# A scaled copy in which most weights are loaded behind the first store, and the first two input tiles are cut differently

## The chip, the cores and the metric

The kernel runs on one core of a Trainium2 chip. A core has several engines with instruction streams of their own: VectorE (DVE), ScalarE (ACT), GpSimd (POOL), SyncE (SP) and TensorE (unused here). Data moves between the chip's main memory (HBM) and the on-chip memory (SBUF, 128 partitions) by DMA: SyncE and ScalarE issue transfers, each into a queue of its own, and 16 DMA engines work both queues off. The metric is the time of one execution on the device in microseconds; lower is better.

## The reference

Every token is a row of 512 numbers and has two weights. The output holds for each token the row times the first weight and the row times the second. The expert indices are not used.

```python
x:              (16, 1024, 512) float32      # 33.6 MB
expert_weights: (16, 1024, 2)   float32      # 0.13 MB
x_expanded = x[:, :, np.newaxis, :].repeat(k, axis=2)     # k = 2
return x_expanded * expert_weights[..., np.newaxis]       # 67.1 MB
```

For each byte read two are written, and one multiplication is made for each output number.

## The kernel before

The 16,384 tokens are laid over 128 partitions, 128 tokens for each. They are cut into five tiles of 25 tokens per partition (L32) and a rest of three (`LAST`, L34). A tile of input is 128 x 51,200 bytes, 6400 KB. Two input buffers exist (`x_pool`, L44), one output buffer for a whole tile (`o_ring`, L48), one small tile for the last three tokens (`z_tile`, L58), and one for all weights (`w_tile`, L47): 256 columns, two for each token.

**Loads.** `load(i)` (L68) issues the input of tile i on ScalarE's queue. Tile 0 comes in two transfers of 9 and 16 tokens (`FIRST`, L35), every other tile in one. Right behind the first transfer of tile 0 the function issues the weights on SyncE's queue in three loads (L95, L97, L104): those of tile 0 (25 KB), of tiles 1 to 4 (100 KB) and of the rest (3 KB). In SBUF a partition's weights of one tile are 200 bytes, so these loads consist of many 200-byte pieces, while a partition's share of an input tile is one piece of 51,200 bytes. Behind tile 0's second transfer comes the input of the last three tokens (L85), then tile 1.

**Products.** `emit` (L148) goes through a tile in parts: the first two tiles in parts of 13 and 12 tokens, the others in 9, 8 and 8 (L157). Each part is filled by `fill` (L142): VectorE takes the first `v` tokens of a part in chunks of up to four (one TENSOR_TENSOR for each, L127), ScalarE the rest with one ACTIVATE for each token and weight (L117). `SHARES` (L36) gives `v`; for the first two tiles ScalarE has four tokens of each part, from the third tile on it has none. When a part is filled, SyncE issues its store (L152).

**Order.** Each engine runs its instructions in the order written. A wait on SyncE or ScalarE holds back every issue behind it on the same engine. The framework adds the waits: a product waits for its input, its weights and for the store that last read its part of `o_ring`; a load into an input buffer waits until all products of the tile that held it before are done. The main loop (L154 to L159) issues loads 0 and 1, then for each tile the products and stores, followed by the load two tiles ahead, on ScalarE behind its products. The last three tokens end the kernel (L160).

Of the kernel before, what the change touches and what calls it, by code (L numbers as in the profile page):

```python
# [1 line left out]

# [4 lines left out]


@with_exitstack
def kernel(  # L10
    ctx: ExitStack,
    tc: tile.TileContext,
    x: bass.AP,
    expert_indices: bass.AP,
    expert_weights: bass.AP,
    out: bass.AP,
):
    nc = tc.nc

    batch, seq, hidden = x.shape  # L20
    k = expert_weights.shape[-1]
    P = nc.NUM_PARTITIONS
    ntok = batch * seq
    assert ntok % P == 0
    A_TOTAL = ntok // P

    f32 = mybir.dt.float32
    row = k * hidden
    CH = 4


    groups = [25, 25, 25, 25, 25]  # L32
    TX = max(groups)
    LAST = 3  # L34
    FIRST = [9, 16]  # L35
    SHARES = [[9, 8], [9, 8], [9, 8, 8]]  # L36
    assert sum(groups) + LAST == A_TOTAL

    xf = x.rearrange("b s h -> (b s) h")
    of = out.rearrange("b s k h -> (b s) (k h)")  # L40
    wf = expert_weights.rearrange("b s k -> (b s) k")

    w_pool = ctx.enter_context(tc.tile_pool(name="w_pool", bufs=1))
    x_pool = ctx.enter_context(tc.tile_pool(name="x_pool", bufs=2))  # L44
    o_pool = ctx.enter_context(tc.tile_pool(name="o_pool", bufs=1))

    w_tile = w_pool.tile([P, A_TOTAL * k], f32)  # L47
    o_ring = o_pool.tile([P, TX * row], f32)  # L48

    def rows(of_all, done, T):  # L50
        return of_all[done * P : (done + T) * P, :].rearrange(
            "(p a) n -> p (a n)", a=T
        )


    if LAST:
        z_pool = ctx.enter_context(tc.tile_pool(name="z_pool", bufs=1))
        z_tile = z_pool.tile([P, LAST * hidden], f32)  # L58

    tiles = []  # L60
    done = 0
    for n in groups:
        tiles.append((done, n))
        done += n

    loaded = []

    def load(i):  # L68
        if i >= len(tiles):
            return  # L70
        done, n = tiles[i]
        x_tile = x_pool.tile([P, TX * hidden], f32)
        src = rows(xf, done, n)
        steps = FIRST if i == 0 else [n]
        for e, step in enumerate(steps):
            at = sum(steps[:e])
            nc.scalar.dma_start(
                out=x_tile[:, at * hidden : (at + step) * hidden],
                in_=src[:, at * hidden : (at + step) * hidden],
            )  # L80
            if i == 0 and e == 0:
                for g in range(3):
                    weights(g)
        if i == 0 and LAST:
            nc.scalar.dma_start(out=z_tile, in_=rows(xf, A_TOTAL - LAST, LAST))  # L85
        loaded.append(x_tile)


    T0 = groups[0]
    G = len([n for n in groups[1:] if n == T0])  # L90
    head = (1 + G) * T0

    def weights(e):
        if e == 0:
            nc.sync.dma_start(out=w_tile[:, : T0 * k], in_=rows(wf, 0, T0))  # L95
        elif e == 1:
            nc.sync.dma_start(  # L97
                out=w_tile[:, T0 * k : head * k].rearrange("p (g n) -> p g n", g=G),
                in_=wf[T0 * P : head * P, :].rearrange(
                    "(g p a) n -> p g (a n)", g=G, p=P  # L100
                ),
            )
        else:
            nc.sync.dma_start(  # L104
                out=w_tile[:, head * k :], in_=rows(wf, head, A_TOTAL - head)
            )

    def product(engine, o_tile, t, x_in, c, m):

        o = t * row  # L110
        if engine is not None:
            for e in range(m * k):
                out_e = o_tile[:, o + e * hidden : o + (e + 1) * hidden]
                in_e = x_in[:, e // k * hidden : (e // k + 1) * hidden]
                w_e = w_tile[:, c + e : c + e + 1]
                if engine is nc.scalar or engine is nc.any and (c + e) % 3 == 2:
                    nc.scalar.mul(out=out_e, in_=in_e, mul=w_e)  # L117
                else:
                    nc.vector.tensor_scalar(
                        out=out_e,  # L120
                        in0=in_e,
                        scalar1=w_e,
                        scalar2=None,
                        op0=mybir.AluOpType.mult,
                    )
            return
        nc.vector.tensor_tensor(  # L127
            out=o_tile[:, o : o + m * row].rearrange(
                "p (t k h) -> p t k h", t=m, k=k
            ),  # L130
            in0=x_in[:, : m * hidden]
            .rearrange("p (t h) -> p t h", t=m)
            .unsqueeze(2)
            .to_broadcast([P, m, k, hidden]),
            in1=w_tile[:, c : c + m * k]
            .rearrange("p (t k) -> p t k", t=m)
            .unsqueeze(3)
            .to_broadcast([P, m, k, hidden]),
            op=mybir.AluOpType.mult,
        )  # L140

    def fill(o_tile, x_in, c, m, v):  # L142
        for t in range(0, v, CH):
            u = min(t + CH, v)
            product(None, o_tile, t, x_in[:, t * hidden : u * hidden], c + t * k, u - t)
        product(nc.scalar, o_tile, v, x_in[:, v * hidden :], c + v * k, m - v)

    def emit(src, dst, c, cuts, shares):  # L148
        for at, to, v in zip(cuts, cuts[1:], shares):
            o_tile = o_ring[:, at * row : to * row]  # L150
            fill(o_tile, src[:, at * hidden : to * hidden], c + at * k, to - at, v)
            nc.sync.dma_start(out=dst[:, at * row : to * row], in_=o_tile)  # L152

    for i in range(2):  # L154
        load(i)
    for i, (done, n) in enumerate(tiles):
        cuts = [0, 13, n] if i < 2 else [0, 9, 17, n]  # L157
        emit(loaded[i], rows(of, done, n), done * k, cuts, SHARES[min(i, 2)])
        load(i + 2)  # L159
    emit(  # L160
        z_tile,
        rows(of, A_TOTAL - LAST, LAST),
        (A_TOTAL - LAST) * k,
        [0, LAST],
        [LAST],
    )

# [1 line left out]
_INS = ['x', 'expert_indices', 'expert_weights']  # L169
_OUTS = [((16, 1024, 2, 512), 'float32')]  # L170


# [23 lines left out]
```

## Time and profile before

| what | before |
|---|---|
| time, median of 3 runs | 239.54 us (239.51 to 239.99) |
| the profiled execution: its time, its span | 240.12 us, 238.3 us |
| bytes read from HBM, written | 33.69 MB, 67.11 MB |
| mean rate over the span | 423 GB/s |
| stores of 6656 KB, 6144 KB (median from issue to landing) | 33.1 us, 44.5 us |

The span runs from the first to the last instruction that the profiler recorded; some time of an execution lies outside it. "Issue to landing" of a transfer holds its wait in the queue as well as its movement. In the lines of issues, ACTq and SPq are the instruction streams of ScalarE and SyncE that issue transfers: the time beside them is that of the issue, and the movement itself comes later.

### The profile page before, as it was taken

What the parts mean: (1) busy time and instruction counts of PE and PEld (TensorE: products, weight loads), DVE (VectorE), ACT (ScalarE), POOL (GpSimd) and SP (SyncE); (2) the same over time, 40 slices, a digit from 0 to 9 for tenths busy, and PEclk for the clock granted to TensorE, in tenths of its full rate; (3) what the DMA queues carried; (4) which work ended last, traced back from release to release, by engine and by line L of the source; (5) the groups of instructions that cost most, each with busy time, mean ns of one, the idle gap of its engine ahead of it and who ended that gap; (6) DMA issues with size and microseconds to landing.
All of it is one profiled execution on the core that took longest, in us unless ns stands there. A gap on an engine that the chain in (4) does not pass through costs nothing.

```text
span 238.3 us, 167 instructions
## 1 busy us (share of the span) xinstructions
DVE 122.6 (51%) x32; ACT 21.2 (9%) x33; POOL 0.2 (0%) x4
## 2 busy tenths in 40 slices
DVE  0599600000069292099405999493086999865000
ACT  0008900000061250000000000000000000000000
POOL 0000000000000000000000000000000000000000
DMA  7999999999999999999999999999999999999996
GB/s 264 465 386 504 457 414 413 413 424 429 429 396 429 472 465 426 422 404 405 412 484 431 402 434 444 414 434 425 449 408 461 434 440 431 421 413 423 440 434 264
DMA packets 3840, 100.80 MB, mean 423 GB/s; under 512 B 1152, under 2 KB 1152, under 8 KB 1280
## 3 DMA queue, kind: packets, MB, share of 16 engines
q1 hardware_dynamic: 2832, 67.24, 65.5%
q10 hardware_dynamic: 1008, 33.55, 33.2%
HBM read 33.69 MB, written 67.11 MB: 423 GB/s over the span
## 4 chain that ended last, share of the span: by engine, by line
DMA 58%; DVE 28%; issue 2%; another core or an unknown queue 2%; ACT 1%; DVEq 0%; SPq 0%
DMA out_dram<-o_ring 55%; DVE o_ring L127 28%; DMA x_tile<-in_x_dram 3%; ACT o_ring L117 1%; DVEq L127 0%; SPq L152 0%
## 5 line engine op out<-in xcount | busy, mean ns | idle before, releaser
L127 DVE TENSOR_TENSOR o_ring<-x_tile,w_tile 128x4096 f32<-128x4096 f32 (+1 forms) x31 | 119.3, 3905 | 93.2 <-DMA out_dram<-o_ring 82.3
L117 ACT ACTIVATE o_ring<-x_tile,w_tile 128x512 f32<-128x512 f32 x32 | 19.9, 708 | 47.1 <-DMA out_dram<-o_ring 47.0
L127 DVE TENSOR_TENSOR o_ring<-z_tile,w_tile 128x3072 f32<-128x3072 f32 x1 | 3.4, 3359 | 2.1 <-DMA out_dram<-o_ring 2.1
L117 ACT ACT_TABLE_LOAD x1 | 1.3, 1283 | 18.7 <-DMA x_tile<-in_x_dram 18.7
L180 POOL MEMSET const-uint8-127<- 128x1 uint8 x1 | 0.1, 102 | 0.0
L180 POOL MEMSET const-bfloat16-1.0<- 128x1 bf16 x1 | 0.1, 101 | 0.0
L180 POOL MEMSET const-float32-0.0<- 128x1 f32 x1 | 0.1, 98 | 0.2 <-issue 0.2
L180 POOL MEMSET const-float32-1.0<- 128x1 f32 x1 | 0.1, 98 | 0.0
## 6 DMA issues: line engine op xcount, KB each, us to landing
x_tile<-in_x_dram ACTq DMA_DIRECT2D x4, 6400.0 KB, 31.6
out_dram<-o_ring SPq DMA_DIRECT2D x6, 4096.0 KB, 21.5
out_dram<-o_ring SPq DMA_DIRECT2D x3, 4608.0 KB, 27.3
out_dram<-o_ring SPq DMA_DIRECT2D x2, 6656.0 KB, 33.1
out_dram<-o_ring SPq DMA_DIRECT2D x2, 6144.0 KB, 44.5
x_tile<-in_x_dram ACTq DMA_DIRECT2D x1, 4096.0 KB, 17.5
x_tile<-in_x_dram ACTq DMA_DIRECT2D x1, 2304.0 KB, 8.1
out_dram<-o_ring SPq DMA_DIRECT2D x1, 1536.0 KB, 19.5
```

What stands on the lines that cost most here:

```text
L117: nc.scalar.mul(out=out_e, in_=in_e, mul=w_e)
L127: nc.vector.tensor_tensor(out=o_tile[:, o : o + m * row].rearrange("p (t k h) -> p t k h", t=m, k=k), in0=x_in[:, : m * hidden] .rearrange ...
L180: nc = _bacc.Bacc("TRN2", target_bir_lowering=False, num_devices=1)
```

## The change

Tile 0 comes in one load and tile 1 in two, of 16 and 9 tokens; the input of the last three tokens follows behind tile 1. The first weight load covers tiles 0 and 1 (50 KB). The other two, of tiles 2 to 4 (75 KB) and of the rest (3 KB), are issued on SyncE behind the first store. To hold them there, ScalarE copies some columns of the input tile into the part of `w_tile` that these loads fill afterwards: the loads must wait for that copy, and the copy stands behind ScalarE's products of the first part. The values copied are overwritten and used by nobody. The shares change too: VectorE takes 7 tokens of each part of tile 0 (ScalarE 6 and 5), and 10 and 9 of tile 1 (ScalarE 3 and 3).

```diff
-    FIRST = [9, 16]
-    SHARES = [[9, 8], [9, 8], [9, 8, 8]]
+    STEPS = {1: [16, 9]}
+    SHARES = [[7, 7], [10, 9], [9, 8, 8]]
...
-        steps = FIRST if i == 0 else [n]
+        steps = STEPS.get(i, [n])
...
             if i == 0 and e == 0:
-                for g in range(3):
-                    weights(g)
-        if i == 0 and LAST:
+                weights(0)
+        if i == 1 and LAST:
             nc.scalar.dma_start(out=z_tile, in_=rows(xf, A_TOTAL - LAST, LAST))
...
     def weights(e):
-        if e == 0:
-            nc.sync.dma_start(out=w_tile[:, : T0 * k], in_=rows(wf, 0, T0))
-        elif e == 1:
+        if e < 2:
+            at, to = ((0, 2 * T0), (2 * T0, head))[e]
+            g = (to - at) // T0
             nc.sync.dma_start(
-                out=w_tile[:, T0 * k : head * k].rearrange("p (g n) -> p g n", g=G),
-                in_=wf[T0 * P : head * P, :].rearrange(
-                    "(g p a) n -> p g (a n)", g=G, p=P
+                out=w_tile[:, at * k : to * k].rearrange("p (g n) -> p g n", g=g),
+                in_=wf[at * P : to * P, :].rearrange(
+                    "(g p a) n -> p g (a n)", g=g, p=P
                 ),
             )
...
             nc.sync.dma_start(out=dst[:, at * row : to * row], in_=o_tile)
+            if c == 0 and at == 0:
+                nc.scalar.copy(
+                    out=w_tile[:, 2 * T0 * k :],
+                    in_=src[:, : (A_TOTAL - 2 * T0) * k],
+                )
+                weights(1)
+                weights(2)
```

## The prediction

> **What bounds the kernel now.** I read the page first: engine shares, the slices and the queues.
>
> ```profile
> DVE 122.6 (51%) x32; ACT 21.2 (9%) x33; POOL 0.2 (0%) x4
> DMA  7999999999999999999999999999999999999996
> DMA packets 3840, 100.80 MB, mean 423 GB/s; under 512 B 1152, under 2 KB 1152, under 8 KB 1280
> q1 hardware_dynamic: 2832, 67.24, 65.5%
> q10 hardware_dynamic: 1008, 33.55, 33.2%
> ```
>
> No compute engine is busy much over half the span, while the 16 DMA engines are full in every slice but the first and the last. Queue q10 carries ScalarE's loads, q1 what SyncE issues: stores and weights. Together they take 98.7% of the engines' time. The split of the span into stages says where the other 1.3% lies (columns: stretch, length, busy time and count for DVE, ACT and POOL, clock, DMA share, GB/s).
>
> ```profile
> 0.00:3.00 3.00, 0.00 (x0) 0.00 (x0) 0.20 (x4) 1.00 0.39 104
> 3.00:20.00 17.00, 11.17 (x4) 1.26 (x1) 0.00 (x0) 1.00 1.06 449
> 20.00:50.00 30.00, 7.45 (x2) 9.93 (x17) 0.00 (x0) 1.00 1.00 421
> 50.00:92.00 42.00, 18.66 (x5) 10.01 (x16) 0.00 (x0) 1.00 1.00 434
> 92.00:150.00 58.00, 36.30 (x10) 0.00 (x0) 0.00 (x0) 1.00 1.00 428
> 150.00:236.00 86.00, 49.05 (x13) 0.00 (x0) 0.00 (x0) 1.00 1.00 431
> 236.00:238.30 2.30, 0.00 (x0) 0.00 (x0) 0.00 (x0) 1.00 0.10 43
> ```
>
> From 3 to 236 us the share is 1.00: the kernel is a transport of fixed bytes at the engines' full rate, with a ramp of about 1.8 us lost ahead (61% of 3 us) and 2.1 behind (90% of 2.3). A wait of DVE, ACT or a store costs nothing as long as either queue still holds work. Only three things can move the end: the ramp, the engine time per byte, and a moment in which both queues are empty.
>
> What lies in the queues early is read from the issues in order of time and their landings (last number: us from issue to landing; the second 6400 KB row is the third tile's load, issued at 29.97).
>
> ```profile
> 0.73 0.89 ACTq L77 DMA_DIRECT2D x_tile<-in_x_dram  x2
> 0.73 0.38 SPq L95 DMA_DIRECT2D w_tile<-in_expert_weights_dram  x1
> 1.64 0.52 ACTq L85 DMA_DIRECT2D z_tile<-in_x_dram  x1
> 2.19 0.81 ACTq L77 DMA_DIRECT2D x_tile<-in_x_dram  x1
> 25.07 193.26 SPq L152 DMA_DIRECT2D out_dram<-o_ring  x14
> 29.97 0.37 ACTq L77 DMA_DIRECT2D x_tile<-in_x_dram  x1
> x_tile<-in_x_dram ACTq DMA_DIRECT2D x1, 2304.0 KB, 8.1
> w_tile<-in_expert_weights_dram SPq DMA_DIRECT2D x1, 25.0 KB, 5.3
> w_tile<-in_expert_weights_dram SPq DMA_DIRECT2D x1, 100.0 KB, 36.7
> x_tile<-in_x_dram ACTq DMA_DIRECT2D x1, 6400.0 KB, 33.8
> x_tile<-in_x_dram ACTq DMA_DIRECT2D x1, 6400.0 KB, 21.8
> out_dram<-o_ring SPq DMA_DIRECT2D x1, 6656.0 KB, 42.4
> ```
>
> A 100 KB load needs 36.7 us. The packets by queue in the stretch from 20 to 36 us say why:
>
> ```profile
> q10 hardware_dynamic: 155, 6.86, 99.5%
> q1 hardware_dynamic: 154, 0.03, 1.0%
> ```
>
> 155 pieces of input went by, and 154 small pieces of SyncE's queue: each engine takes **one piece from each queue in turn**, whatever its size. Each transfer has one piece for each of 128 partitions, 8 per engine; the weights are 8+32+8 = 48 per engine. These stand before the first store in SyncE's queue. So the store issued at 25.07 cannot move until the third tile's load has landed (29.97+21.8 = 51.8), and it lands at 67.5. The reader should see that this block is real but free: the engines carry loads meanwhile.
>
> The Trainium skill, "DMA: Bandwidth & Descriptors", section "Queues, rings and completion order", lets an engine drain a whole packet, some 9 to 17 descriptors, before it changes queue; by that the weights would pass in a few turns. The 155 against 154 speaks against it here.
>
> **The change, part by part.** Bytes and packets first. Before: 7 loads, 3 weight loads, 14 stores. After: 7 loads (tile 0 in one, tile 1 in two), 3 weight loads, 14 stores, with 16, 24 and 8 weight pieces per engine in place of 8, 32 and 8. Pieces per engine and bytes are equal: **0**. The ramp: the first load and first weight load are both issued at 0.73 as before: **0**.
>
> The one price that shows in the queue rows is that loads run less smoothly than stores: 67.24 MB in 65.5% of 238.3 us is 431 GB/s, 33.55 MB in 33.2% is 424. At the stores' rate the loads would need 77.9 us rather than 79.1, so **1.2 us** is the whole excess. It cannot be placed from these rows, but stages that start or mix loads show lower rates. The change adds a mixed stage (the first store meets the second tile's pieces) and moves others. Ends: -1.2 if all excess went, +1.2 if it doubled; I take +0.1, near nothing, since from the fourth load on everything meets the same partners as before.
>
> Now the schedule, as that decides whether a queue runs empty. Prices of compute:
>
> ```profile
> L127 DVE TENSOR_TENSOR o_ring<-x_tile,w_tile 128x4096 f32<-128x4096 f32 x26 | 113.8, 4421 | 93.2 <-DMA out_dram<-o_ring 82.3 <-DMA x_tile<-in_x_dram 8.8 <-issue 2.1
> L127 DVE TENSOR_TENSOR o_ring<-x_tile,w_tile 128x1024 f32<-128x1024 f32 x5 | 6.1, 1219 | 0.0
> L127 DVE TENSOR_TENSOR o_ring<-z_tile,w_tile 128x3072 f32<-128x3072 f32 x1 | 3.4, 3359 | 2.1 <-DMA out_dram<-o_ring 2.1
> 18.74 1.28 ACT L117 ACT_TABLE_LOAD   x1 [18.74 <-DMA x_tile<-in_x_dram]
> 20.03 9.91 ACT L117 ACTIVATE o_ring<-x_tile,w_tile 128x512 f32<-128x512 f32 x16
> ```
>
> *The first tile in one load.* Its bytes are the same, so it lands at 18.7, as its second part did (18.74); the loss is DVE's early start at 8.8. *The first weight load* now has 16 pieces and a completion mark per engine, 17 turns. How many pass before input starts moving? In the old profile a 2304 KB load is 8 pieces of 0.70 us (2.359 MB at 424 GB/s, an eighth); it landed at 8.8, the weights at 6.0, so some 4 of the 8 turns lay behind them. Of 9 weight turns, 4 alternated and 5 went ahead. With 5 ahead again, 12 alternate: 8 with the first tile's pieces, 1 with its completion mark, 3 with the second tile's 32 KB pieces (4.194 MB at 424 GB/s, an eighth: 1.24 us). So the weights land not with the tile but at 18.7 + 3 x 1.24 = **22.4**, and all of DVE and ACT waits for them. The table load lies under that wait.
>
> *New shares.* Seven tokens on DVE: 4.42 + 3.36 = 7.8 us; six on ACT: 12 x 0.62 = 7.4. First store issued at 30.2 rather than 25.07. ScalarE's queue holds the first two tiles and the last three tokens, 13.9 MB as before, until the old landing of the second tile, 2.19 + 33.8 = 36.0; I take 35.4 for the last byte moved (an estimate). From an issue to its first piece:
>
> ```profile
> 0.73 8.08 DMA x_tile<-in_x_dram
> q10 hardware_dynamic: 4, 0.07, 66.0%
> q1 hardware_dynamic: 44, 0.01, 18.0%
> ```
>
> The last two rows are the stretch from 1.5 to 2.0 us, in which the first four input pieces and 44 of SyncE's moved: 0.8 to 1.3 us behind the issue at 0.73, I take 1.1. The store moves from 31.3: **cover of 4 us** is left. Cost 0.
>
> *Copy and late weights.* The copy writes 156 columns on ACT, between none and 0.62 us (one 512-column ACTIVATE); I take 0.3, as 156 is under a third. A change of table there and back would add 2 x 1.28. Behind it on ACT stand ten products (6.2 us) and the issue of the third tile's load. ACT ends at 29.8 + 0.3 + 6.2 = 36.3, at most 39.2; DVE ends its second seven tokens at 30.2 + 7.8 = 38.0. SyncE waits for the copy with two small loads, and the second store is queued behind them, ready only at 38.0 anyway. The third tile's load is issued at about 38, not 29.97; the first store covers it: **0**, and if it were not there, 38.0+1.1-35.4, some 4 us, would be idle.
>
> *What is late next.* The first store's 6.82 MB take 15.8 us at 431 GB/s; in its 8 turns it meets three 18 KB pieces (0.70 each) and five of the last tokens' pieces (0.23): 31.3 + 15.8 + 2.1 + 1.2 = 50.4, against 67.5 before. DVE's ten tokens of tile 1 (2 x 4.42 + 2.3, between the 1219 and the 3359 row) end at 61.5. The late weights again alternate with 8 big pieces, now the third tile's (15.5 us, to 67), then 25 small ones pass, then the second store (6.29 MB, 14.6 us) lands near 82. Before:
>
> ```profile
> 67.59 9.90 DVE o_ring L127 x3
> 77.49 4.48 another core or an unknown queue
> 82.06 8.77 DVE o_ring L127 x2
> 90.89 0.36 ACTq L77 DMA_DIRECT2D x_tile<-in_x_dram  x1
> ```
>
> There the second store freed its half at 82.0 too. So the 17 us won at the first store are given back in a longer wait for the second. Tile 1's second half: 9 tokens, 9.9 us, and the fourth load is issued near 92 against 90.89; the third store (15.8 us from 82) covers it with 6 us to spare. From there the two kernels are alike.
>
> **Sum:** 238.3 + 0 + 0 + 0.1 = 238.4 of span, about 240.2 for the execution, which took 240.12 with 1.8 outside its span. The median of the runs is 239.54, 0.6 lower; differences are added to that: **239.6**.
>
> **Rivals.** *Starved (slower).* The first store waits for weights, and the weights for turns. If no weight piece goes ahead of the input on one engine (their generation takes longer with 16 pieces than with 8, and all 16 engines must finish), 17 turns alternate: five more of 1.24 us, landing at 28.6, first store moving at 37.5, and both queues are empty from 35.4: 2.1 us, all lost. With one ahead it is 0.9; from two ahead on nothing. Time 240.4 to 241.6, middle 241.1. For it: the pieces double and the lead was only 5. Against it: 44 of SyncE's pieces against 4 of input moved from 1.5 to 2.0 us. Chance 0.20.
>
> *Switching dearer (slower).* Store and load meet once more, and the excess of 1.2 us over five large loads grows by half or more: +0.6 to +1.2, 240.3. Against it: the stretch 92 to 150, where loads mix with stores, still shows 428 GB/s. Chance 0.13.
>
> *Smoother loads (faster).* The big pieces at the beginning and the small weights out of the way remove half or all of the excess: -0.6 to -1.2, 238.7. For it: the stretch 20 to 50 has the lowest rate of the middle, 421, and is the one that changes. Against it: the same number of weight pieces still alternates with input. Chance 0.15.
>
> *It does not do what it says.* If weights pass many to a turn, they land with the tile, the first store is issued at 26.5, and nothing starves either. By the rule of the Trainium skill ("DMA: Bandwidth & Descriptors", the section above) this is what happens. Same 239.6; it is held in the forecast.
>
> **How the numbers follow.** A measurement of this kernel can tell about 0.2% (0.48 us) from no change. Forecast, no change: 0.52, between 239.1 and 240.0. Slower 0.20 + 0.13 = 0.33, faster 0.15. For 8 in 10 the range reaches to 238.9 (most of the smooth case, whose full end is 238.3) and to 241.6 (the end of the starved case).
>
> **What would show it.** Right: DMA share of 1.00 in every stage from 3 to 236 us; DVE's first instruction near 22.5, some 4 us after the tile has landed; the first store landing near 50, the second near 82; the fourth load issued near 92. Starved: DVE's first instruction past 27 and a hole in the DMA slices near 36. Smoother or dearer: shares of 1.00 but q10's share of time below 32.8% or above 33.5% for the same 33.55 MB. I would be wrong altogether if the ramp moved: a first slice other than 7.

## The result, and the profile after

| | before | after |
|---|---|---|
| median of 5 runs each | 239.56 us (239.51 to 239.99) | 246.44 us (246.38 to 250.33) |
| ratio to before, 95% interval | 1 | 1.0292 (1.0267 to 1.0317) |
| execution shown: time, span | 240.12, 238.3 us | 246.35, 244.2 us |

The changed kernel is 2.9% slower: 6.9 us, where the forecast was 239.6 us and the range ended at 241.6. The first profile of the changed kernel was taken in a disturbed execution of 250.33 us, so the rows of "after" come from a repeat of the same kernel (run e16 below).

The page of the changed kernel, first: engine shares, slices, queues.

```profile
span 244.2 us, 174 instructions
DVE 121.5 (50%) x32; ACT 22.7 (9%) x36; POOL 0.2 (0%) x4
DMA  7999969799999999999999999999999999999995
DMA packets 3840, 100.80 MB, mean 413 GB/s; under 512 B 1152, under 2 KB 1152, under 8 KB 1280
q1 hardware_dynamic: 2832, 67.24, 64.5%
q10 hardware_dynamic: 1008, 33.55, 32.5%
```

Packets and bytes are those of before, to the digit. The engines work 97.0% of 244.2 us, 236.9 us in all, against 98.7% of 238.3, 235.2. So 4.2 of the 5.9 us of span are time in which engines stand still, and the rest is longer engine time for the same bytes. The slices show where to look: a 6 in the sixth and a 7 in the eighth, from 30 to 49 us, and a 5 in the last. The split into stages is sharper (columns as in the prediction):

```profile
0.00:3.00 3.00, 0.00 (x0) 0.00 (x0) 0.20 (x4) 1.00 0.88 273
3.00:34.00 31.00, 5.13 (x2) 5.14 (x8) 0.00 (x0) 1.00 0.96 410
34.00:36.00 2.00, 2.00 (x1) 2.00 (x4) 0.00 (x0) 1.00 0.53 215
36.00:38.30 2.30, 2.30 (x2) 2.30 (x5) 0.00 (x0) 1.00 0.00 0
38.50:60.00 21.50, 5.67 (x2) 5.45 (x9) 0.00 (x0) 1.00 1.03 402
60.00:236.00 176.00, 106.19 (x28) 7.57 (x12) 0.00 (x0) 1.00 1.00 431
```

A row credits a piece to the stretch in which it begins, with its whole time and bytes, so a share can pass 1, and the edges of a stretch shift its rate; the rate divided by the share is free of that.

From 36.0 to 38.3 us no piece begins (by the trace's records the last one had ended at 35.7), and both compute engines are busy throughout. This is the moment of two empty queues that the prediction named as one of three things that could move the end. From 60 us on the rate is 431 GB/s, as before: nothing is won or lost there until the last microseconds. The stretch between, 38.5 to 60, has full engines (1.03) and yet moves 402 GB/s, where before it was 427 at 1.02:

```profile
38.50:60.00 21.50, 0.00 (x0) 0.00 (x0) 0.00 (x0) 1.00 1.02 427
```

Divided by the share that is 390 against 419 GB/s. The timeline says what was late:

```profile
0.73 1.39 ACTq L77 DMA_DIRECT2D x_tile<-in_x_dram  x3
0.73 0.44 SPq L96 DMA_DIRECT2D w_tile<-in_expert_weights_dram  x1
28.84 1.28 ACT L116 ACT_TABLE_LOAD   x1 [28.84 <-DMA w_tile<-in_expert_weights_dram]
28.87 15.30 DVE L126 TENSOR_TENSOR o_ring<-x_tile,w_tile 128x4096 f32<-128x4096 f32 x4 [28.87 <-DMA w_tile<-in_expert_weights_dram]
37.62 0.35 SPq L151 DMA_DIRECT2D out_dram<-o_ring  x1
44.26 0.36 ACTq L77 DMA_DIRECT2D x_tile<-in_x_dram  x1
64.28 10.96 DVE L126 TENSOR_TENSOR o_ring<-x_tile,w_tile 128x4096 f32<-128x4096 f32 x3 [20.11 <-DMA out_dram<-o_ring]
88.18 9.90 DVE L126 TENSOR_TENSOR o_ring<-x_tile,w_tile 128x4096 f32<-128x4096 f32 x3 [12.94 <-issue]
98.16 49.17 ACTq L77 DMA_DIRECT2D x_tile<-in_x_dram  x2
```

The bracket behind DVE's first instruction reads: idle for 28.87 us, and a weight load ended it. The chain of waits has the same (start, us, what):

```profile
0.73 28.04 DMA w_tile<-in_expert_weights_dram
28.87 15.31 DVE o_ring L126 x4
44.23 28.81 DMA out_dram<-o_ring
```

A load of 50 KB is on the path for 28 us. The packets by queue, first from 1.5 to 2.0 us, say how it began:

```profile
q10 hardware_dynamic: 11, 0.56, 374.9%
```

There is no row for q1: eleven input pieces had begun, and not one piece of weights. From 5 to 15 us:

```profile
q10 hardware_dynamic: 81, 4.15, 95.7%
q1 hardware_dynamic: 81, 0.02, 0.8%
```

One for one again. Sixteen pieces and a completion mark, each behind a big piece of input: no weight piece went ahead. The Trainium skill, "DMA: Bandwidth & Descriptors", section "Queues, rings and completion order", lets an engine drain a whole packet of some 9 to 17 descriptors before it changes queue; 81 against 81 does not agree with it, and by it the weights would have landed with the first tile or before it.

### The profile page after: what moved, and what is told of

Its sections match the earlier page's. It is cut to its first block, busy times and chain, and to the rows that moved or that the text cites. A ratio compares the mean times of both kernels' runs of the same rounds, so it can differ in the third digit from the quotient of the medians.

```text
span 248.2 us, 174 instructions
## 1 busy us (share of the span) xinstructions
DVE 121.5 (49%) x32; ACT 22.7 (9%) x36; POOL 0.2 (0%) x4
## 4 chain that ended last, share of the span: by engine, by line
DMA 68%; DVE 19%; issue 4%; SPq 0%; DVEq 0%
DMA out_dram<-o_ring 57%; DVE o_ring L126 19%; DMA w_tile<-in_expert_weights_dram 11%; SPq L151 0%; DVEq L126 0%
## 5 line engine op out<-in xcount | busy, mean ns | idle before, releaser
L126 DVE TENSOR_TENSOR o_ring<-x_tile,w_tile 128x4096 f32<-128x4096 f32 (+3 forms) x31 | 118.1, 3869 | 104.2 <-DMA out_dram<-o_ring 52.8
L116 ACT ACTIVATE o_ring<-x_tile,w_tile 128x512 f32<-128x512 f32 x34 | 21.3, 708 | 40.2 <-DMA out_dram<-o_ring 40.2
L116 ACT ACT_TABLE_LOAD x1 | 1.3, 1283 | 28.8 <-DMA w_tile<-in_expert_weights_dram 28.8
## 6 DMA issues: line engine op xcount, KB each, us to landing
out_dram<-o_ring SPq DMA_DIRECT2D x6, 4096.0 KB, 22.4
```

The lines of the kernel that those rows point to most:

```text
L126: nc.vector.tensor_tensor(out=o_tile[:, o : o + m * row].rearrange("p (t k h) -> p t k h", t=m, k=k), in0=x_in[:, : m * hidden] .rearrange ...
```

## The experiments

Each was compared with runs of the kernel before on the same chip; those medians were 240.03 to 240.22 us. "Slower" in the text means that the interval of the ratio lies above 1.

### Is it the late weights?

**e5** repeats the changed kernel beside three variants; **e6** issues the first weight load on ScalarE's queue, ahead of the first tile; **e7** issues all three weight loads at the start, without the copy; **e8** leaves the kernel before as it is and only gives ScalarE ten tokens in place of four in the first tile's second part, so that the third tile's load is issued late.

> The changed kernel itself. If its first weight load is always late (16 pieces that all wait behind input pieces), DVE's first instruction is again near 29 us and both queues are empty from about 36 to 38.5; 246 to 247 us. If that was chance, some executions are near 243, what the version with two first weight loads takes.

e6, against the changed kernel:

```diff
+            if i == 0 and e == 0:
+                weights(0, nc.scalar)
             nc.scalar.dma_start(
...
-            if i == 0 and e == 0:
-                weights(0)
...
```

> The changed kernel with its first weight load (two tiles, 16 pieces) on ScalarE's queue ahead of the first input, so that no input piece can stand before it. Weights land by 4 us, tile 0 by 19.5, the first store is issued near 27, no hole. 'Empty queues' as the whole cause: 239.5 to 240.5. What the split weights showed (242.3 to 243.7 without the hole): half of the loss comes from elsewhere, so 242 to 244 again.

e7, against the changed kernel:

```diff
-                weights(0)
+                for g in range(3):
+                    weights(g)
...
-            if c == 0 and at == 0:
-                nc.scalar.copy(
-                    out=w_tile[:, 2 * T0 * k :],
-                    in_=src[:, : (A_TOTAL - 2 * T0) * k],
-                )
-                weights(1)
-                weights(2)
```

> The changed kernel with its two later weight loads at the start, behind the first one, and no copy. If the first load's 16 pieces lose their turn to the 51,200-byte input pieces whatever follows them: DVE starts near 29 us, the hole is there, 245 to 247. If they go ahead, as 18,432-byte pieces let them in the kernel before: no hole, 241 to 243 like the single first load alone.

e8, against the kernel before:

```diff
-    SHARES = [[9, 8], [9, 8], [9, 8, 8]]
+    SHARES = [[9, 2], [9, 8], [9, 8, 8]]
```

> The kernel before with only one number changed: in tile 0's second part VectorE takes 2 tokens and ScalarE 10, so that the third tile's load is issued near 37.4 instead of 30 us, when ScalarE's queue has just run dry (near 36) and the first store has begun to move. No moment with both queues empty. Theory 'load queue running dry costs' (the engines stall when a load comes into an empty queue beside moving stores): 241 to 243, with the stalls between 37 and 45 us. 'Only empty queues cost': 239.5 to 240.3.

| | median (range), runs | ratio (95%) | DVE begins |
|---|---|---|---|
| e5 | 246.45 (245.94 to 247.09), 4 | 1.0259 (1.0224 to 1.0294) | 28.80 |
| e6 | 242.32 (241.31 to 243.39), 4 | 1.0086 (1.0039 to 1.0134) | 19.57 |
| e7 | 245.52 (245.16 to 246.02), 4 | 1.0220 (1.0188 to 1.0252) | 28.74 |
| e8 | 239.98 (239.72 to 240.27), 4 | 0.9988 (0.9958 to 1.0018) | 8.84 |

All four ran on one chip. With the weights ahead of the input, 4.1 us of the loss are gone (246.45 - 242.32). Moving the other weight loads back to the start gives at most a microsecond; the intervals of e5 and e7 overlap. In e8 the stage from 38.5 to 60 us reads

```profile
38.50:60.00 21.50, 0.00 (x0) 0.00 (x0) 0.00 (x0) 1.00 1.00 433
```

Its third tile's load was issued at 37.5 instead of 29.97, into a queue that had run dry, while a store moved, and nothing was lost. So an empty load queue alone does no harm. e6 also shows a rest: with no hole (no moment of two empty queues) the kernel is still 0.9% slower than before, 2.3 us.

### The parts alone

Five variants of the kernel before, each with one or two parts of the change. **e2**: only the first weight load covers two tiles. **e4**: only the late weights (those of tiles 1 to 4 and the rest, behind the first store). **e11**: only the first tile in one load. **e12**: only the second tile in two pieces. **e10**: only the new shares of the second tile.

e2, against the kernel before; e4 has the changed kernel's copy and late loads, from column `T0 * k` on:

```diff
-        if e == 0:
-            nc.sync.dma_start(out=w_tile[:, : T0 * k], in_=rows(wf, 0, T0))
-        elif e == 1:
+        if e < 2:
+            at, to = ((0, 2 * T0), (2 * T0, head))[e]
+            g = (to - at) // T0
...
```

> The kernel before, with only its first weight load widened to two tiles (16 pieces per engine) and the second narrowed to three; all weights still at the start, input as before. Both theories: the first weights land near 18 us instead of 6 if none of the 16 goes ahead of the input (near 13 if five do), DVE starts that much later, second part of tile 0 done near 37.6; the queue of loads lasts to 36 and the first store then stands ready, so no hole: 239.5 to 240.0. More than 241 would say that the late start costs by another way than empty queues.

> The kernel before with only the late weights of the change: tile 0's weights at the start (8 pieces), those of tiles 1 to 4 and of the rest behind the first store, held by the copy; input and shares as before. First store issued near 25 and moving from about 26 while the loads still run to 36 and longer: no hole, but early mixing. 'Empty queues': 239.5 to 240.0. 'Mixing': 241.5 to 243.5.

e11:

```diff
-    FIRST = [9, 16]
-    SHARES = [[9, 8], [9, 8], [9, 8, 8]]
+    FIRST = [25]
+    SHARES = [[7, 7], [9, 8], [9, 8, 8]]
```

> The kernel before with only tile 0 in one load and shares of 7 and 7 for it; tile 1 in one load behind the last three tokens, its shares as before, weights at the start. 'Shares': 239.6 to 240.5. 'Cut of the input', if it is the single first load: 241.5 to 243.

e12 (and the last three tokens' load behind tile 1):

```diff
-    FIRST = [9, 16]
+    STEPS = {0: [9, 16], 1: [16, 9]}
...
-        steps = FIRST if i == 0 else [n]
+        steps = STEPS.get(i, [n])
```

> The kernel before with only tile 1 in loads of 16 and 9 tokens and the last three tokens behind it; all else as before. 'Shares': 239.6 to 240.5. 'Cut of the input', if it is the second tile's cut or the small load of the last tokens beside the first store: 241.5 to 243.

e10:

```diff
-    SHARES = [[9, 8], [9, 8], [9, 8, 8]]
+    SHARES = [[9, 8], [10, 9], [9, 8, 8]]
```

> The kernel before with only tile 1's shares changed to 10 and 9. 'Shares': 241.5 to 243, stalls near 95 to 102. 'Cut of the input': 239.6 to 240.3.

| | median (range), runs | ratio (95%) |
|---|---|---|
| e2 | 240.14 (239.58 to 242.58), 10 | 1.0020 (0.9993 to 1.0048) |
| e4 | 239.86 (239.62 to 240.29), 10 | 0.9992 (0.9980 to 1.0005) |
| e11 | 240.24 (239.99 to 241.15), 10 | 1.0008 (0.9989 to 1.0028) |
| e12 | 242.98 (240.30 to 251.23), 4 | none: runs 240.30, 240.45, 245.51, 251.23 |
| e10 | 241.03 (240.26 to 242.24), 10 | 1.0039 (1.0015 to 1.0063) |

e4 and e11 cost nothing: late weights with their copy, and the first tile in one load, are free. In e4 the first store moves beside the loads as early as 26 to 34 us (22 of its pieces begin there), so the early mixing that its expectation and that of e1 name as a rival is not the cause either. e2 costs nothing either, but there DVE began at 9.30 and the 50 KB had landed in 8.5 us: on that chip, beside a first input load of nine tokens, the bigger weight load did go ahead, so e2 says nothing of the step in question. e12 stays open: two of its four runs are far off, the other two are near the kernel before.

The surprise is e10. Moving two tokens of the second tile from ScalarE to VectorE costs 1.0 us (241.03 - 240.07, the kernel before on that chip), though ScalarE is idle for nine tenths of the time and VectorE for nearly half of it. The time lies between the two ranges of the expectation: the shares cost something, but less than was thought. The last two stages of e10,

```profile
236.00:237.00 1.00, 0.00 (x0) 0.00 (x0) 0.00 (x0) 1.00 0.35 148
237.00:240.00 3.00, 0.00 (x0) 0.00 (x0) 0.00 (x0) 1.00 0.03 12
```

and of the kernel before,

```profile
236.00:237.00 1.00, 0.00 (x0) 0.00 (x0) 0.00 (x0) 1.00 0.24 98
237.00:240.00 3.00, 0.00 (x0) 0.00 (x0) 0.00 (x0) 1.00 0.00 0
```

differ in a thin tail: a share of 0.03 over 3 us is as much as one engine of sixteen for 1.4 us (0.03 x 3 x 16). The other engines have ended by then. Why the shares of an early tile make one engine late at the end is not settled.

### Combinations

**e3** has the input cuts and the shares of the change with the weights as before; **e9** is e3 with the old shares [9, 8] of the second tile. **e1** is the changed kernel with the first weight load as two loads of one tile; **e14** is e1 with the old shares.

e3, against the kernel before; e9 has [9, 8] for [10, 9]:

```diff
-    FIRST = [9, 16]
-    SHARES = [[9, 8], [9, 8], [9, 8, 8]]
+    STEPS = {1: [16, 9]}
+    SHARES = [[7, 7], [10, 9], [9, 8, 8]]
...
-        if i == 0 and LAST:
+        if i == 1 and LAST:
```

> The kernel before with only the input and the shares of the change: tile 0 in one load, tile 1 in 16 and 9 tokens, the last three tokens behind it; weights in three loads at the start as before. 'Empty queues': tile 0's weights (8 pieces) land by about 10 to 19 us, first store issued near 27.5, third input load issued near 34.3, before the loads run out: 239.5 to 240.0. 'Mixing': the small weights again hold the first store back until the third tile has landed, so no early mixing: 239.5 to 240.0 too. Over 241 would say that the single first load costs by itself.

> The kernel of e3 (input and shares of the change, all weights at the start), but with tile 1's shares as before (VectorE 9 and 8 tokens, not 10 and 9). Theory 'shares': with 9 tokens DVE needs 9.9 us for tile 1's second part instead of 8.8, so the fourth load and the fourth store are issued about 1 us later beside the third store, and that is where e3 stalled (95 to 102 us); then 239.6 to 240.5 here. Rival 'cut of the input' (one big first load, or tile 1 in two): 241.5 to 243 as e3.

e1, against the changed kernel:

```diff
-                weights(0)
+                weights(0, 0, T0)
+                weights(0, T0, 2 * T0)
...
```

> The changed kernel, its first weight load (16 small pieces per DMA engine) issued as two loads of one tile each (8 pieces, then 8). Theory 'empty queues' (the time is lost while neither queue holds work, because the first products wait for 16 pieces that move one per input piece): tile 0's weights need 9 turns at most, so they land by about 19 us; the first store is issued near 27.5 and moves long before the loads end near 35.5; no hole; 239.5 to 240.0 us. Rival 'mixing' (stores that move while loads still run slow both, and that is half of the loss or more): the hole is gone, but stores still meet loads early, so 242.5 to 243.5.

> The changed kernel with both repairs: its first weight load in two loads of one tile each (no hole) and tile 1's shares as before. If lateness of the weights and the new shares are all that costs: 240.0 to 240.8, the same as before within 0.3%. If single big loads or weights behind the first store cost too: 241.5 or more.

| | median (range), runs | ratio (95%) |
|---|---|---|
| e3 | 242.31 (240.79 to 246.28), 8 | 1.0090 (1.0054 to 1.0126) |
| e9 | 240.50 (239.82 to 242.21), 10 | 1.0021 (0.9996 to 1.0047) |
| e1 | 243.22 (242.29 to 243.74), 4 | 1.0128 (1.0097 to 1.0159) |
| e14 | 241.92 (240.01 to 244.71), 4 | 1.0102 (1.0031 to 1.0172) |

e3 is slower than the kernel before by 0.9%, and e9 with the old shares cannot be told from it. That points to the shares again, but e3 and e9 ran on different chips and e3's runs scatter over 5 us, so the 1.8 us between them are no measure of the price. e1 has no hole (DVE begins at 18.90) and is 3.2 us faster than the changed kernel, but still slower than before; in e14 the runs scatter too far to say whether the old shares help there. e1 and e14 ran on chips on which a two-tile load went first as well (e2, e13), so their times don't show that splitting it is what put the weights ahead.

### Who goes first, and what it costs

**e13** is the changed kernel with the old shares of the second tile. It ran on a chip on which the weights went ahead. **e16** and **e17** are the changed kernel and e13 once more, side by side on another chip. **e18** is e13 with the 3 KB weight load ahead of the first one on SyncE, so that the first weights are forced to come later.

e13 (and e17), against the changed kernel:

```diff
-    SHARES = [[7, 7], [10, 9], [9, 8, 8]]
+    SHARES = [[7, 7], [9, 8], [9, 8, 8]]
```

> The changed kernel with tile 1's shares as before (VectorE 9 and 8 tokens, not 10 and 9); the late first weights stay. If the empty queues and the stalls right behind them cost about 4 us and the new shares some 2: DVE starts near 29 us, the hole near 36 is there, 243.5 to 244.8. If the empty queues are nearly all of it: 245.5 to 246.5. If the shares are the larger part: 242 to 243.

> The changed kernel once more, on the same chip and beside e17, which differs in tile 1's shares alone. In its traces so far the first input piece moved at 1.79 us and no weight piece before 4.1; in the kernel of e13 the weights went first at 1.77 and the input at 1.95, though both issue the same two first transfers at the same time. If who goes first belongs to the program (a few nanoseconds in its start): weights late again, hole near 36, 246 to 247. If it belongs to the chip: as e17 beside it, 242 to 243.5 if the weights go first on this chip.

> The changed kernel with tile 1's old shares, once more. If who goes first belongs to the program: weights first, DVE from about 19.4 us, no hole, 240.5 to 242. If it belongs to the chip and the input goes first on this one: DVE from about 29, hole near 36, 243.5 to 245.

e18, against e13:

```diff
+                weights(2)
                 weights(0)
...
-                    out=w_tile[:, 2 * T0 * k :],
-                    in_=src[:, : (A_TOTAL - 2 * T0) * k],
+                    out=w_tile[:, 2 * T0 * k : head * k],
+                    in_=src[:, : (head - 2 * T0) * k],
                 )
                 weights(1)
-                weights(2)
```

> The changed kernel with tile 1's old shares and the first weight load made late for certain: the 3 KB load of the last weights stands ahead of it on SyncE's queue, so its issue begins some 0.45 us behind the first input load. Its 16 pieces per engine then all wait behind input pieces: DVE from 29 to 31 us, first store issued near 38 to 40, both queues empty from about 36 for 3 to 5 us. If the hole and the restart behind it are the larger part of the loss: 243.5 to 246.5. If late weights cost little and the new shares are the cause: 240.5 to 242.

| | median (range), runs | ratio (95%) | DVE begins |
|---|---|---|---|
| e13 | 241.35 (240.48 to 242.30), 10 | 1.0040 (1.0018 to 1.0062) | 19.41 |
| e16 | 246.64 (246.35 to 247.08), 4 | 1.0266 (1.0240 to 1.0292) | 28.87 |
| e17 | 245.69 (245.62 to 245.95), 4 | 1.0227 (1.0204 to 1.0250) | 28.83 |
| e18 | 247.87 (247.63 to 247.99), 4 | 1.0314 (1.0291 to 1.0337) | 30.89 |

e13 and e17 are the same program, 4.3 us apart, while the kernel before took 240.22 and 240.20 us on the two chips. The timeline of e13 has DVE wait for the weights only until 19.41:

```profile
19.41 15.30 DVE L126 TENSOR_TENSOR o_ring<-x_tile,w_tile 128x4096 f32<-128x4096 f32 x4 [19.41 <-DMA w_tile<-in_expert_weights_dram]
28.16 0.35 SPq L151 DMA_DIRECT2D out_dram<-o_ring  x1
```

and its packets from 1.5 to 2.0 us read

```profile
q10 hardware_dynamic: 3, 0.15, 95.9%
q1 hardware_dynamic: 60, 0.01, 45.0%
```

Sixty weight pieces had begun against three of input, where e16 had none against eleven. The same 50 KB landed after 18.6 us in e13 and after 28.0 in e17. What differs besides the chip is which of two transfers, issued at the same 0.73 us, began first.

The chip is not all. In e18, on the chip of e17 and with the same input, the first load on SyncE is the one of 3 KB, with 8 pieces per engine in place of 16. From 1.5 to 2.0 us its pieces did begin first:

```profile
q10 hardware_dynamic: 4, 0.20, 131.8%
q1 hardware_dynamic: 53, 0.00, 5.0%
```

The trace's records give the time of the first piece of each queue. In all twelve traces in which SyncE's first load has 8 pieces per engine, the first small piece began at 1.71 to 1.73 us, ahead of the input at 1.78 to 1.95, whether the small pieces held 24, 200 or 1,024 bytes and those of input 18,432 or 51,200. With 16 pieces it began at 1.77 (e13) and 1.79 (e2) where it led. Where it lost (e5, e7, e16, e17 and the first profile of the changed kernel), the input began at 1.78 or 1.79 and the weights at 4.1 to 4.4. So a load of two tiles starts some 0.06 us later than one of one tile, just when the input starts, and the order becomes a close race. Why it falls out differently on different chips, and whether the later start comes from the number of pieces or from the form of the load (two tiles need one more dimension), was not tested.

The pages show what that costs. Span and queues of e13, then of e17:

```profile
span 238.5 us, 176 instructions
q1 hardware_dynamic: 2832, 67.24, 65.5%
q10 hardware_dynamic: 1008, 33.55, 33.1%
```

```profile
span 243.9 us, 176 instructions
q1 hardware_dynamic: 2832, 67.24, 64.6%
q10 hardware_dynamic: 1008, 33.55, 32.6%
```

The engines work 98.6% of 238.5 = 235.2 us in e13 and 97.2% of 243.9 = 237.1 in e17; they stand still for 3.3 and 6.8. So of the 5.4 us between the spans (these two executions took 240.61 and 245.68), 3.5 are the hole and 1.9 are **slower work on the same bytes**. The stages of e17 say where:

```profile
34.00:38.50 4.50, 4.50 (x2) 4.50 (x9) 0.00 (x0) 1.00 0.50 204
38.50:60.00 21.50, 5.63 (x2) 5.40 (x9) 0.00 (x0) 1.00 0.98 380
60.00:236.00 176.00, 103.99 (x27) 10.02 (x16) 0.00 (x0) 1.00 1.00 432
```

From 38.5 to 60 the engines are full at 380 GB/s (388 divided by the share; e13 has 427 at 0.99, which is 431). Its packets from 40 to 44 us,

```profile
q1 hardware_dynamic: 32, 1.70, 98.8%
```

and from 46 to 50 us,

```profile
q1 hardware_dynamic: 22, 1.17, 103.1%
q10 hardware_dynamic: 10, 0.51, 36.3%
```

give the time of one store piece: 0.988 x 16 x 4 / 32 = 1.98 us at first, and 1.031 x 16 x 4 / 22 = 3.00 us some 8 us behind the hole, as the third tile's load comes in. In e13 the stores' pieces of 46 to 50 us took 1.97 us (32 in 98.3%). The traces of e5 and e16 have 2.99 us in the same place, and e18, whose hole ends 2 us later, has it from 48 to 52 us. But slower pieces also come without a hole. In the kernel before, the loads' pieces took 1.90 us from 40 to 44 us and 2.19 from 46 to 50. In e6, which has no hole, the engines work 98.1% of 241.2 us, 236.6 in all, nearly as long as in e17, with the slow pieces spread over the whole span.

e18 puts a slope to it: DVE begins 2.06 us later than in e17, and the time is 2.18 longer. Nothing covers lateness here. The times of e17 and e18 lie above the ranges of their expectations (245 and 246.5): the price of lateness was taken too low once more.

### Another way to get the weights early

**e15** lays the tokens out so that a partition's 128 tokens lie together in HBM; then all weights are one load with one 1,024-byte piece for each partition.

```diff
-        return of_all[done * P : (done + T) * P, :].rearrange(
-            "(p a) n -> p (a n)", a=T
-        )
+        n = of_all.shape[-1]
+        return of_all.rearrange("(p a) n -> p (a n)", p=P)[
+            :, done * n : (done + T) * n
+        ]
...
-                for g in range(3):
-                    weights(g)
+                weights()
...
```

> The kernel before with another layout: each partition holds 128 tokens that lie together in memory, so that all weights come in one load of 1,024-byte pieces, 8 per DMA engine in place of 48, and the first store has 8 pieces before it. Input and output pieces keep their sizes. As the engines are busy throughout, 40 pieces of about 16 ns less are 0.6 us: 239.0 to 239.6. If partitions that lie 256 KB (input) and 512 KB (output) apart slow the transfers: over 240.5.

It took 244.77 us (243.95 to 245.03, 4 runs), ratio 1.0176 (1.0141 to 1.0210): slower. All 128 KB of weights had landed in 7.4 us, so that aim was met, but the large transfers lost: from 26 to 64 us it moved

```profile
26.00:64.00 38.00, 2.12 (x1) 4.51 (x8) 0.00 (x0) 1.00 0.99 393
```

that is 393 GB/s, and the kernel before in the same stretch

```profile
26.00:64.00 38.00, 1.45 (x1) 3.94 (x7) 0.00 (x0) 1.00 0.98 416
```

416 with engines that are as full. The first store moves earlier in e15, but so it does in e4, which has 417 GB/s in this stretch. What else changed is the distance in HBM from one partition's piece to the next: 50 KB became 256 KB for the loads, and 100 KB became 512 KB for the stores. The Trainium skill, "DMA: Bandwidth & Descriptors", section "Latency and other measured facts", has copies between HBM tensors slow down at row pitches of large powers of two (207 GB/s in each direction at 512 KB, where a padded pitch had 214); the loss of 1.8% here agrees with it in kind, though no run here padded the pitch to show that it is the cause.

No version that was run beats both kernels; e4, e8 and e11 equal the one before.

## Why the prediction was wrong

**The bound** was read rightly: engines full from end to end, and only the ramp, the engine time per byte and empty queues can move the end. All that happened is on that list. A small misreading has no consequence: as a stage row credits whole pieces to where they begin (hence its 1.06), the 1.8 and 2.1 us of ramp add up to more than the 3.1 us that 98.7% of 238.3 leave.

**One piece from each queue in turn** held (155 : 154 before, 81 : 81 after). Likewise the count of 17 turns.

**"With 5 ahead again, 12 alternate"** is the step that failed. It put the landing at 22.4 us; it was 28.8. The lead of 5 turns was worked out for a load of 8 pieces per engine and carried over to one of 16, as if the start of the weights did not depend on the load. It does: loads of 8 began at 1.71 to 1.73 us and always led, that of 16 came into a tie with the input near 1.79, and in every trace of the changed kernel itself it lost, so that all 17 turns alternated. Nor was 5 right where it led: in e13 142 small pieces against 29 of input had begun by 5 us, 7 turns more on each of 16 engines, and the weights landed at 19.3. The row that the prediction held against the starved rival, 44 of SyncE's pieces against 4 of input by 2.0 us, belonged to the old load of 8. And "cover of 4 us" was counted from the landing so found.

**The table load "lies under that wait"** was wrong too. ACT_TABLE_LOAD stands at 28.84, behind the same weights. ACT's part takes 1.28 + 7.46 us and so ends at 37.6, later than DVE's 7.8 us would (36.7): the first store lost another microsecond.

**The starved rival** (0.20, 240.4 to 241.6) had the mechanism: no piece ahead, 17 turns, landing at 28.6. Its two signs came, DVE's first instruction past 27 (28.87) and a hole near 36; of the signs for the forecast none did (the first store landed at 64.2 in place of 50, the second at 88.1 in place of 82, and the fourth load was issued at 98.16 in place of 92), though the ramp held, with its first slice of 7. Its price of 2.1 us was too small. The runs show 4.1 (e5 - e6, one chip) and 4.3 (e17 - e13; 5.1 between the two executions in the profile). The hole was 3.5: the table load moved its end, and the input ran out earlier and engine by engine, with a share of 0.53 from 34 to 36 us. The 1.9 us of slower work were in no term of the sum. It shows from 46 to 54 us, behind the hole, but why pieces are slow there is not settled: a load that enters a dry queue beside a moving store isn't enough (e8), and e6 has slower work without a hole.

**The excess of loads, +0.1**, held the other two losses, and "a wait of DVE, ACT or a store costs nothing as long as either queue still holds work" does not hold for the shares, though no queue ran empty. New shares of the second tile: +1.0 (e16 - e17, e10 - before). The rest: 1.1, which is e13 against before, 0.4% (0.18 to 0.62); of its parts, one load for tile 0 and late weights are free alone (e11, e4), and the cut of the second tile (e12) is unclear. Together 4.3 + 1.0 + 1.1 = 6.4 (e16, 246.64 - 240.20); as these are steps along one chain of kernels, they must add up. A check from outside the chain is e6, which has no hole and loses 2.3 us (242.32 - 240.03), about the last two together.

**The copy** was right: COPY took 0.3 us, with no second table load. Its wait and the late weight loads were right at 0 (e4). "The 17 us won at the first store are given back" could not show in the changed kernel, whose first store landed at 64.2, against 67.5 before. e13 shows it, with the weights early:

```profile
51.84 9.90 DVE L126 TENSOR_TENSOR o_ring<-x_tile,w_tile 128x4096 f32<-128x4096 f32 x3 [17.14 <-DMA out_dram<-o_ring]
82.47 5.01 ACT L116 ACTIVATE o_ring<-x_tile,w_tile 128x512 f32<-128x512 f32 x8 [25.66 <-DMA out_dram<-o_ring]
91.38 49.98 ACTq L77 DMA_DIRECT2D x_tile<-in_x_dram  x2
```

The first store landed near 51.8 (forecast 50.4), the second near 82.5 (82), and the fourth load was issued at 91.38 (92). So the schedule that the prediction drew was right for weights that land early, and even then the kernel was 0.4% slower than before.

## What to carry to other kernels

When a transfer of many small pieces shares the engines with one of large pieces, its landing time is turns times the large piece's time; ask what happens if it loses the first turn, and price that case above the hole alone (here 4.3 us for a hole of 3.5). A lead that was read from one transfer is not a constant: don't carry it to one of twice the pieces, and put what everything waits for ahead of the input on the same queue (e6: 242.32 against 246.45 us). Where a time is set by transfers, a token moved between engines that are not the limit may still cost something; measure it.

## What the runs showed of the hardware that was not expected

- Of two transfers issued within the same 0.01 us on two queues, which begins first was not the same on all chips: the same program had its 50 KB of weights after 18.6 us on one and 28.0 on another, and took 241.35 and 245.69 us. On each chip it was the same in all four to ten runs, as far as their times tell.
- The start of a transfer depends on the transfer: the first small piece began at 1.71 to 1.73 us for loads of 8 pieces per engine and at 1.77 and 1.79 for one of 16, issued at the same 0.73 us.
- A hole in which both queues are empty went with a loss above its length: 3.5 us of idle engines, and 1.9 us of longer work on the same bytes, seen some 8 us behind the hole, where store pieces took 3.00 us instead of 1.98. The cause is open.
- The last microsecond belongs to the slowest of 16 engines: e10 has the bytes and nearly the engine time of the kernel before, and ends 1.3 us later in span (239.6 against 238.3).
